# A two-layer hybrid encoder on one core: the four buffers of the sums of x at other addresses by 256 than the weights

## The chip, the core and the metric

The kernel runs on one core of one Trainium2 chip. The metric is the device time of one execution in microseconds (us), the median of several runs. Of the core's engines, the profile calls the matrix engine PE, and the part of it that loads the stationary operand PEld; VectorE is DVE, ScalarE is ACT, GpSimd is POOL, and SP issues most DMAs. All operands of a matmul lie in the on-chip memory, in 128 partitions. An address below is a byte offset inside a partition.

## The reference

Two layers work on 256 tokens of width 1024, all in float32. Each layer has a half-weighted SwiGLU block, an attention block with two groups of heads, and a second SwiGLU block. Shortened:

```python
def swiglu(h, w_gate, w_up, w_down):
    return (jax.nn.silu(h @ w_gate) * (h @ w_up)) @ w_down

for l in range(DEPTH):                      # 2
    x = x + 0.5 * swiglu(rms_norm(x, ffn1_norm[l]), ffn1_w_gate[l], ffn1_w_up[l], ffn1_w_down[l])
    h = rms_norm(x, mix_norm[l])
    qa, ka, va, qb, kb, vb = jnp.split(h @ w_in[l], SPLITS, axis=-1)
    out_a = windowed_gqa_sink(qa, ka, va, sink[l], slopes_a)
    out_b = differential_attention(qb, kb, vb, lam, slopes_b)
    out_b = (rms_norm(out_b, diff_subln[l]) * (1.0 - lam_init)).reshape(b, s, B_V_COLS)
    x = x + jnp.concatenate([out_a, out_b], axis=-1) @ w_out[l]
    x = x + 0.5 * swiglu(rms_norm(x, ffn2_norm[l]), ffn2_w_gate[l], ffn2_w_up[l], ffn2_w_down[l])
return rms_norm(x, final_norm)
```

The hidden width of a SwiGLU block is 2816: five groups of 512 columns and a rest of 256.

## The kernel before

**Matmuls in two halves.** Every float32 operand is split into a high and a low half of type float32r, which PE multiplies in one pass. A product a·b is three matmuls into one accumulator: high·high, low·high, high·low. The weights come by DMA into `raw` tiles of 8 KB a partition (six of them) and are split there by ScalarE (the cast to the high half) and VectorE (the difference to the low one) into tiles `w` of 4 KB. These share the pool `s4` (28 tiles) with the halves of x and of the hidden blocks, which are named `s` in the profile. In the SwiGLU blocks the activations are the stationary operand (128 columns, 512 bytes) and the weights the moving one (512 columns, 2 KB). PEld loads the next matmul's stationary operand while the present one streams.

**Seven products in place of eight.** For most groups of 512 columns `by_sevens` computes the gate and up projections of both token blocks by a scheme with seven products instead of eight: x and the weights are cut in two along the tokens and along the 1024 inputs, and sums of parts are multiplied. Four of the seven products take a sum of parts of x as the stationary operand. The three others take a quarter of x itself (`quarter`, in the pool `s4`). `make_sums` forms the four sums once per norm, and `high` and `low` write their halves: three of them into tiles with the tag `q` (three buffers), one into a tile with the tag `v` (one buffer). `summed(i)` hands them to `prod`, which issues 12 matmuls of 512 columns for one sum:

```python
        def prod(xo, w, acc=None):
            ...
                pe.matmul(acc, lhsT=xh, rhs=hi, start=first and k == 0, stop=False, skip_group_check=not first)
                pe.matmul(acc, lhsT=xl, rhs=hi, start=False, stop=False, skip_group_check=not first)
                pe.matmul(acc, lhsT=xh, rhs=lo, start=False, stop=k == 3, skip_group_check=not first)
```

Fifteen groups in the four SwiGLU blocks go this way (three in the first block, four in each other): 15 x 4 x 12 = 720 matmuls whose stationary operand is a sum.

**The same buffers in the attention block.** There the sums are not alive. `q_finish` puts the halves of the projected queries into the buffers with the tag `q`, and `scores` loads them as stationary operand in 64 rows, two matmuls side by side, against the keys (`blk()`, pool `s4`). `vB`, the values of the second head group, lies in the buffer with the tag `v` and is the moving operand of the product with the attention weights.

**Order.** PE's instructions stay in the order of the program; `ahead` and the tables `LEAD` say how early a weight is fetched and split. A scheduler that knows durations places the rest. None of that depends on an address.

**Where tiles lie.** A pool's tags follow one another in the order of their first use; a tag with n buffers takes n tiles in a row, each rounded up to 32 bytes. Taken modulo 256, the `raw` tiles, all tiles of `s4`, the five buffers of the tag `tmp`, and the buffers of `q` and `v` begin at 160; x itself (`xk`) and the identity (`ident`) begin at 128, `vA` at 32. Within a tile the operands start at multiples of 512 bytes. Behind `v` in the same pool lie small tiles of the attention block (`den_b`, `R`, `negm`, `vA` and others).

Of the kernel before, what the change touches and what calls it, by code (L numbers as in the profile page):

```python
# [9 lines left out]
F32 = mybir.dt.float32  # L10
F32R = mybir.dt.float32r
# [3 lines left out]
P = 128  # L15
# [31 lines left out]
def trunk(ctx: ExitStack, tc: tile.TileContext, x, n1, g1, u1, d1, nm, w_in, sink,  # L47
# [26 lines left out]
    tp = ctx.enter_context(tc.tile_pool(name="tp", bufs=1))  # L74
# [4 lines left out]
    def nm_(s):  # L79
        uid[0] += 1  # L80
        return f"{s}_{uid[0]}"
# [4 lines left out]
    def pair():  # L86
        return [ps.tile([P, 512], F32, tag="xy", bufs=2, name=nm_("xy")) for _ in range(2)]
# [6 lines left out]

    def tmp(tag="tmp", bufs=5, shape=(P, 2, 256), dt=F32):
        return tp.tile(list(shape), dt, tag=tag, bufs=bufs, name=nm_(tag))

    f = lambda t: t.bitcast(F32)

    def urgent():  # L100

        return tc.high_priority(300)
# [241 lines left out]
    class Norm:  # L344


        def __init__(self, g0, sums=True):
            self.g0, self.xs, self.sums = g0, [], sums
            self.xg, self.turned = [], []
            self.ss = tmp("nss", 2, (P, 2, 4))  # L350

        def squares(self, t, c, n):
            j_ = tmp("junk", 1, (P, 512))
            act.activation(j_[:, :n], xk[:, t, c:c + n], AF.Square, accum_out=self.ss[:, t, c // 256:c // 256 + 1])
# [34 lines left out]
        def make_sums(self):  # L389

            self.sm = []

            (t0, t1), (b0, b1) = [(t[:, :, 0:P], t[:, :, P:S]) for t in self.xg]

            def add(x, y, op):
                v = tmp().rearrange("p a (c s) -> p (a c) s", c=2)
                dve.tensor_tensor(v, x, y, op=op)
                return v

            def high(v):  # L400
                tag, n = ("q", 3) if len(self.sm) < 3 else ("v", 1)
                sm = tp.tile([P, 2, 512], F32R, tag=tag, bufs=n, name=nm_(tag)).rearrange("p a (c s) -> p (a c) s", c=2)
                act.copy(sm[:, :, 0:P], v)
                self.sm.append(sm)

            def low(i, v):
                dve.tensor_tensor(self.sm[i][:, :, P:S], v, f(self.sm[i][:, :, 0:P]), op=ALU.subtract)

            v = add(t1, t0, ALU.subtract)
            s1 = add(t1, b1, ALU.subtract)  # L410
            yield
            high(v)
            high(s1)
            yield
            low(0, v)
            s2 = add(t0, s1, ALU.subtract)
            low(1, s1)
            b0_ = add(b0, s2, ALU.subtract)
            yield
            high(b0_)  # L420
            high(s2)
            yield
            low(2, b0_)
            low(3, s2)
            yield
# [8 lines left out]
        def summed(self, i):  # L434
            return lambda k: (self.sm[i][:, k, 0:P], self.sm[i][:, k, P:S])
# [191 lines left out]
    def split(dst, src, scale=None):  # L627

        act.copy(dst[:, :, 0:S], src)
        dve.tensor_tensor(dst[:, :, S:512], src, f(dst[:, :, 0:S]), op=ALU.subtract)  # L630
# [331 lines left out]
    def mix(l, norm, nxt_norm):  # L962
# [10 lines left out]
        def whole(sl, sc=(1.0, 1.0)):  # L973

            t = tmp()
            for i, b in enumerate(sl):
                act.activation(t[:, i], b[:, S:512], AF.Copy, scale=sc[i])
            for i, b in enumerate(sl):
                dve.scalar_tensor_tensor(t[:, i], in0=b[:, 0:S], scalar=sc[i], in1=t[:, i], op0=ALU.mult, op1=ALU.add)
            dve.tensor_tensor(t, t, bc(norm.R), op=ALU.mult)  # L980
            return t

        def q_finish(sl, sc):
            q = tp.tile([P, 2, 512], F32R, tag="q", bufs=3, name=nm_("q"))
            with urgent():
                split(q, whole(sl, sc))
            return [q[:, 0], q[:, 1]]
# [54 lines left out]
        k_finish(whole(s0), 2, [("b", 0), ("b", 1)])  # L1042
        k_finish(whole(s1), 2, [("b", 2), ("b", 3)])
        q0 = q_finish(ngroup(norm, weights()), [qscB[:, 0:1], qscB[:, 1:2]])
        q1 = q_finish(ngroup(norm, weights()), [qscB[:, 2:3], qscB[:, 3:4]])
        tkv = whole(ngroup(norm, weights()))
        a_b = [soft_b(0, q0[0]), soft_b(1, q0[1])]
        k_finish(tkv, 1, ["a"])

        qA0 = q_finish(ngroup(norm, weights()), [qscA[:, 0:1], qscA[:, 1:2]])  # L1050
        a_b += [soft_b(2, q1[0]), soft_b(3, q1[1])]
        vsl = halves(bank())
# [16 lines left out]
        def keys_first_b(hp):  # L1069
            return keys_first(lambda kc, i: a_b[2 * hp + i // 2][:, i % 2, kc * P:(kc + 1) * P])  # L1070
# [3 lines left out]


        aT = [keys_first_b(0)]
        vB = tp.tile([P, 2, 512], F32, tag="v", bufs=1, name=nm_("v"))
        both = pair()
        vsl = both
        for k0 in (0, 4):  # L1080
# [123 lines left out]
    for l in range(DEPTH):  # L1204
        final = l == DEPTH - 1
        parts = ffn(norm, attention_constants, take_x, sevens=SEVEN[0]) if l == 0 else ffn(norm)
        norm_m = Norm(16 + l * 8, False)
        ffn_close(parts, norm_m)
        norm2 = Norm(32 + l * 8)
        mix(l, norm_m, norm2)  # L1210
        parts = ffn(norm2, final_gain if final else None, final=final)
        if not final:
            norm = Norm((l + 1) * 8)
            ffn_close(parts, norm)
# [75 lines left out]
```

## Time and profile before

| what | value |
|---|---|
| median of 3 runs | 909.28 us (909.23 to 909.46) |
| profiled execution, first to last instruction (span) | 907.5 us |
| granted clock of PE, mean | 0.999 |
| PE busy, its share of the span | 899.1 us, 99% |
| PEld / DVE / ACT / POOL busy | 751.0 / 785.9 / 609.8 / 63.2 us |
| share of PE in the chain of work that ended last | 98% |
| HBM read | 199 MB, 220 GB/s over the span |

The profiled execution has no other time of its own than the span; the median of the runs is 1.8 us above it.

A row of instructions names the output and the inputs by the program's tiles without their numbers: `ps<-w,q` is a matmul into a tile of the tag `ps`, with a weight `w` and a tile of the tag `q` as operands; then the rows and columns of the array in use, the shape of the moving operand, the count, the busy time in us, the mean of one in ns, and the idle time of the engine before them with what ended it. All rows have line 62, the line of the helper that issues for every engine, so groups are told apart by tile names. A matmul's recorded time ends after its result has drained, so consecutive matmuls overlap in the record, and the pace is read from their starts or from many of them together. The chain of waits follows the work that ended last back from the end, step by step.

### The profile page before, as it was taken

How to read it: one execution, taken by the hardware profiler on the slowest of the kernel's cores; microseconds unless marked ns; L12 is line 12 of the kernel's file. 1: busy time of each engine (PE TensorE's matmuls, PEld its weight loads, DVE VectorE, ACT ScalarE, POOL GpSimd, SP SyncE). 2: the span in 40 equal slices, each digit the busy share in tenths (PEclk: the TensorE clock that was granted, in tenths of full speed). 3: DMA queues.
4: the chain of work that ended last, by engine and by line, in shares of the span. 5: the costliest groups of instructions: out<-in, count | busy, mean ns of one | idle time of the engine just before them, and what ended most of it. 6: DMA issues, size and time to landing. Idle time of an engine off the chain costs nothing.

```text
span 907.5 us, 12030 instructions
## 1 busy us (share of the span) xinstructions
PE 899.1 (99%) x4468; PEld 751.0 (83%) x4468; DVE 785.9 (87%) x1069; ACT 609.8 (67%) x970; POOL 63.2 (7%) x79
## 2 busy tenths in 40 slices
PE   9999999999999999999999999999999999999997
PEld 7888888888888888888888888888888888888886
DVE  5968999879987899999778999988888978999894
ACT  6946677666776776677575776667667785776660
POOL 0401000000001001000000001000000000101011
PEclk9999999999999999999999999999999999999999
DMA  9998897954148798897976898899611786898731
GB/s 328 355 287 213 236 309 247 268 143 179 47 150 241 174 265 247 247 300 256 279 204 171 250 278 258 252 303 248 182 57 48 263 223 166 234 312 255 219 114 47
DMA packets 114331, 200.83 MB, mean 221 GB/s; under 512 B 3678, under 2 KB 31648, under 8 KB 114272
## 3 DMA queue, kind: packets, MB, share of 16 engines
q1 hardware_dynamic: 97616, 167.66, 54.4%
q0 software_dynamic: 16096, 31.75, 20.1%
q8 instruction: 35, 0.57, 0.2%
q10 hardware_dynamic: 560, 0.66, 0.2%
q14 instruction: 24, 0.20, 0.1%
HBM read 199.00 MB, written 1.05 MB: 220 GB/s over the span
## 4 chain that ended last, share of the span: by engine, by line
PE 98%; DMA 1%; issue 0%; SPq 0%; DVE 0%; POOLq 0%; POOL 0%
PE ps L62 73%; PE xy L62 25%; DMA xk<-in_x_dram 1%; SPq L172 0%; DVE s L62 0%; DVE xk L62 0%; POOLq L1285 0%; POOL rf L62 0%; SPq L469 0%; SPq L465 0%; DVE tot L62 0%; DVE tmp L62 0%
## 5 line engine op out<-in xcount | busy, mean ns | idle before, releaser
L62 DVE TENSOR_TENSOR w<-raw,w 128x1024 fp32r<-128x1024 f32 (+1 forms) x458 | 476.4, 1097 | 34.6 <-ACT w L62 33.2
L62 PE MATMUL ps<-w,s 128*128 128x512 f32 (+1 forms) x2046 | 473.6, 389 | 0.0
L62 PEld LDWEIGHTS ps<-w,s 128*128 128x128 f32 x2046 | 379.9, 188 | 78.7 <-issue 0.8
L62 ACT CAST w<-raw 128x1024 fp32r<-128x1024 f32 (+1 forms) x457 | 403.9, 954 | 54.0 <-DVE raw L62 38.7
L62 PE MATMUL xy<-w,s 128*128 128x512 f32 x528 | 125.8, 392 | 0.0
L62 PEld LDWEIGHTS xy<-w,s 128*128 128x128 f32 x528 | 98.2, 188 | 20.4
L62 PE MATMUL xy<-w,q 128*128 128x512 f32 x360 | 88.1, 393 | 0.0
L62 PEld LDWEIGHTS xy<-w,q 128*128 128x128 f32 x360 | 66.5, 188 | 13.3
L62 PE MATMUL ps<-s,w 128*128 128x512 f32 (+1 forms) x384 | 69.8, 338 | 0.0
L62 DVE TENSOR_TENSOR raw<-raw,raw 128x2048 f32<-128x2048 f32 x30 | 68.6, 2288 | 0.5
L62 POOL DMA_DIRECT2D raw<-in_ffn_w_up_dram x30 | 38.9, 1313 | 430.1 <-DVE w L62 264.9
L62 PEld LDWEIGHTS ps<-s,w 128*128 128x128 f32 x384 | 58.6, 188 | 8.5
L62 ACT ACTIVATE s<-ps,gcol 128x256 fp32r<-128x256 f32 (+1 forms) x80 | 31.4, 479 | 34.0 <-PE ps L62 34.0
L62 ACT CAST s<-ps 128x512 fp32r<-128x512 f32 x36 | 20.4, 592 | 43.2 <-PE ps L62 43.0
L62 PE MATMUL ps<-w,q 128*128 128x512 f32 x180 | 43.2, 389 | 0.0
L62 PE MATMUL ps<-w,v 128*128 128x512 f32 x180 | 43.2, 389 | 0.0
L62 DVE TENSOR_TENSOR s<-ps,s 128x512 fp32r<-128x512 f32 x36 | 24.1, 686 | 19.5 <-ACT s L62 19.3
L62 PEld LDWEIGHTS ps<-w,v 128*128 128x128 f32 x180 | 33.8, 188 | 7.0
L62 PEld LDWEIGHTS ps<-w,q 128*128 128x128 f32 x180 | 33.8, 188 | 7.0
L62 ACT ACTIVATE s<-s,negm 128x256 f32<-128x256 f32 x64 | 31.8, 498 | 5.3 <-DVE negm L62 5.3
L62 ACT COPY ps<-ps 128x512 f32<-128x512 f32 x15 | 8.6, 570 | 34.4 <-PE ps L62 34.4
L62 DVE SCALAR_TENSOR_TENSOR s<-ps,gcol,s 128x256 fp32r<-128x256 f32 x48 | 20.3, 477 | 13.0 <-ACT s L62 12.9
(131 smaller groups left out, 584.3 us busy)
## 6 DMA issues: line engine op xcount, KB each, us to landing
raw<-in_ffn_w_down_dram SPq DMA_DIRECT2D x44, 1024.0 KB, 7.0
raw<-in_ffn_w_gate_dram SPq DMA_DIRECT2D x39, 1024.0 KB, 7.7
raw<-in_ffn_w_up_dram SPq DMA_DIRECT2D x39, 1024.0 KB, 7.1
raw<-in_ffn_w_up_dram POOLq DMA_DIRECT2D x30, 1024.0 KB, 10.0
raw<-in_w_in_dram SPq DMA_DIRECT2D x14, 1024.0 KB, 6.7
raw<-in_ffn_w_gate_dram SPq DMA_DIRECT2D x8, 512.0 KB, 7.9
raw<-in_ffn_w_up_dram SPq DMA_DIRECT2D x8, 512.0 KB, 8.9
raw<-in_w_in_dram SPq DMA_DIRECT2D x8, 512.0 KB, 6.0
```

What stands on the lines that cost most here:

```text
L62: ins = issue(*a, **k)
```

## The change

The tiles of the sums are made by a new helper, `summed`. The tag `q` gets tiles of 1048 columns instead of 1024, of which the first 1024 are used, so that its three buffers lie 4192 bytes apart. Ahead of the first buffer of each tag stands a tile that nothing uses, of 32 bytes for `q` and 96 bytes for `v`. By that the three buffers of `q` begin 32, 128 and 224 bytes behind the weights' address by 256, and the one of `v` 160 bytes behind. What follows `v` in the pool lies 416 bytes further on. The three places that made these tiles call the helper. The instructions are the same.

```diff
+    placed = set()
+
+    def summed(tag, n, dt=F32R):
+
+        if tag not in placed:
+            placed.add(tag)
+            tp.tile([P, 8 if tag == "q" else 24], F32, tag="edge_" + tag, bufs=1, name="edge_" + tag)
+        t = tp.tile([P, 1024 + 24 * (tag == "q")], dt, tag=tag, bufs=n, name=nm_(tag))
+        return t[:, 0:1024].rearrange("p (a n) -> p a n", a=2)
...
             def high(v):
                 tag, n = ("q", 3) if len(self.sm) < 3 else ("v", 1)
-                sm = tp.tile([P, 2, 512], F32R, tag=tag, bufs=n, name=nm_(tag)).rearrange("p a (c s) -> p (a c) s", c=2)
+                sm = summed(tag, n).rearrange("p a (c s) -> p (a c) s", c=2)
                 act.copy(sm[:, :, 0:P], v)
...
         def q_finish(sl, sc):
-            q = tp.tile([P, 2, 512], F32R, tag="q", bufs=3, name=nm_("q"))
+            q = summed("q", 3)
...
-        vB = tp.tile([P, 2, 512], F32, tag="v", bufs=1, name=nm_("v"))
+        vB = summed("v", 1, F32)
```

## The prediction

> **What bounds the kernel now.** I read the page's first and fourth parts first, to see which engine sets the end.
>
> ```profile
> span 907.5 us, 12030 instructions
> PE 899.1 (99%) x4468; PEld 751.0 (83%) x4468; DVE 785.9 (87%) x1069; ACT 609.8 (67%) x970; POOL 63.2 (7%) x79
> PEclk9999999999999999999999999999999999999999
> PE 98%; DMA 1%; issue 0%; SPq 0%; DVE 0%; POOLq 0%; POOL 0%
> ```
>
> The matrix engine is the path: 98% of the chain of waits, at a clock that never drops. So an edit pays only if a matmul on PE, or the load of its stationary operand (PEld), takes another time. The change issues the same instructions, so the only question is what an address does to one. Next come the groups of PE's instructions with their shapes kept apart.
>
> ```profile
> L62 PE MATMUL ps<-w,s 128*128 128x512 f32 x2010 | 469.3, 390 | 0.0
> L62 PE MATMUL xy<-w,q 128*128 128x512 f32 x360 | 88.1, 393 | 0.0
> L62 PE MATMUL ps<-s,w 128*128 128x512 f32 x192 | 68.2, 398 | 0.0
> L62 PE MATMUL ps<-w,q 128*128 128x512 f32 x180 | 43.2, 389 | 0.0
> L62 PE MATMUL ps<-w,v 128*128 128x512 f32 x180 | 43.2, 389 | 0.0
> L62 PE MATMUL ps<-s,q 64*128 64x256 f32 x144 | 10.7, 289 | 0.0
> L62 PE MATMUL ps<-s,vA 128*64 128x256 f32 x64 | 7.3, 382 | 0.0
> ```
>
> The sums of x (q and v) are the stationary operand of 360 + 180 + 180 = 720 matmuls, the weights (w) their moving operand. The mean of one row hides gaps, so the chain of waits in order of time gives the true pace: start, length, instructions.
>
> ```profile
> 41.28 10.88 PE xy L62 x48
> ...
> 100.20 10.88 PE ps L62 x48
> ```
>
> 10.88 us / 48 = 226.7 ns from one start to the next, and the recorded 389 ns is that pace plus 162 ns in which the result drains beside the next matmul. 720 x 226.7 ns = 163 us, 18% of the span, is all that the sums' loads lie beneath.
>
> **The change part by part.** Nothing is removed and no wait is added. Three things move: the four buffers of the sums, the small tiles allocated behind them, and so the distance between what PE loads and what it streams.
>
> First, what is the distance now? By the sizes of the pools, taken in order and each tile rounded up to 32 bytes, the raw weights, the blocks of the split weights and of x, tmp, q and v all start at 160 modulo 256: relation 0 throughout. xk and ident start at 128, which is 224 from the weights. The table by tile for q, in the stretch 107.6 to 120 us, shows how even relation 0 is (shortest, median and longest ns):
>
> ```profile
> L62 PE MATMUL ps<-w,q x12: 389/389/389, 108.2 to 110.7; 128*128 128x512 f32 x12
> L62 PE MATMUL xy<-w,q x12: 389/389/389, 110.9 to 113.4; 128*128 128x512 f32 x12
> ```
>
> q lies 256 bytes off the weights modulo 512 and the halves of x lie 0 off; both take 389 ns. So a distance of 256 does nothing. That is why only the remainder by 256 can count, and no row here shows 32, 128 or 160 beneath this kind of matmul.
>
> The largest gain that a better relation can bring is the cost of the load itself: no relation is better than no load. The trace has such a matmul. At 232.55 us the last matmul ahead of the scores streams with no load beneath it, because the next stationary operand (64 rows of q) is loaded only after it. The first two lines are the load engine's timeline around it, the third the groups in 232.80 to 232.86 us, where this matmul is alone.
>
> ```profile
> 231.88 0.64 PEld L62 LDWEIGHTS xy<-w,s 128*128 128x128 f32 x3
> 232.87 0.65 PEld L62 LDWEIGHTS ps<-s,q 64*128 64x128 f32 x10 [0.35 <-issue]
> L62 PE MATMUL xy<-w,s 128*128 128x512 f32 x1 | 0.4, 388 | 0.0
> ```
>
> 388 ns without a load against 389 with one: at relation 0 a load costs the stream 1 ns. Gain at most 720 x 1 ns = 0.7 us. With the shortest of 360 in the row below (387) it would be 720 x 2 = 1.4 us.
>
> ```profile
> L62 PE MATMUL xy<-w,q x360: 387/389/497, 66.4 to 860.7; 128*128 128x512 f32 x180
> ```
>
> The Trainium skill (TensorE: Matmul & The Clock Gate, Step-by-step: what each phase is for) says that PE reads the streamed and the loaded operand through two independent ports and that "Loading the next tile's weights doesn't steal SBUF read bandwidth from the running matmul." By that rule the change gives exactly nothing; the 388 against 389 agrees to 1 ns.
>
> The rule of two free ports is not the whole of it, though. Another relation does appear once under a 512-column matmul: where transposes follow, the load of xk (224) or of a hidden block s (0) rides beneath the last matmul. Both windows below hold one matmul alone, 277.65 to 277.68 us with xk loaded, 160.72 to 160.77 us with s:
>
> ```profile
> L62 PE MATMUL ps<-w,s 128*128 128x512 f32 x1 | 0.4, 392 | 0.0
> ...
> L62 PE MATMUL xy<-w,s 128*128 128x512 f32 x1 | 0.4, 395 | 0.0
> ```
>
> Relation 224 is 3 ns shorter than relation 0 here. It is a load in transpose form, so its price (4 to 7 ns over 388) is not that of an ordinary load; but it shows a load can stretch the stream, and gives the loss's bounds. If an ordinary load at a new relation cost 4 ns instead of 1, the sum is 720 x 3 = 2.2 us; with 7 instead of 1, 720 x 6 = 4.3 us. The dearest mean in the trace for 512 columns is 398 (weights stationary, two sizes in turn), still at relation 0: 720 x 9 = 6.5 us, the far end. I take 0, because an ordinary load is nearest to the 388/389 pair, and keep -1.4 and +6.5.
>
> The scores use q as stationary operand too, in 64 rows, two at a time. Here are the shortest, median and longest, then the attention product with v moving, then the one with vA:
>
> ```profile
> L62 PE MATMUL ps<-s,q x144: 275/278/383, 214.1 to 686.1; 64*128 64x256 f32 x144
> L62 PE MATMUL xy<-s,q x48: 276/280/280, 215.0 to 668.9; 64*128 64x256 f32 x48
> L62 PE MATMUL xy<-v,s x64: 275/275/275, 247.2 to 696.6; 128*128 128x128 f32 x64
> L62 PE MATMUL ps<-s,vA x64: 379/379/430, 252.7 to 701.8; 128*64 128x256 f32 x64
> ```
>
> 192 score matmuls are 96 pairs; median over shortest is 3 to 4 ns, so at most 96 x 4 = 0.4 us either way. v as moving operand: 64 without any spread, 0. vA, which the longer buffers push 416 bytes on, already lies off its partner (32 against 160) and its median is its shortest: 0.
>
> The sums are written by ScalarE and VectorE. xk at 224 stands for a shifted operand:
>
> ```profile
> L62 DVE TENSOR_TENSOR q<-tmp,q 128x512 fp32r<-128x512 f32 x20 | 13.7, 684 | 2.9 <-ACT q L62 2.9
> L62 DVE TENSOR_TENSOR xk<-xk,ps 128x512 f32<-128x512 f32 x17 | 11.2, 681 | 2.2 <-PE ps L62 2.2
> ```
>
> 681 against 684 ns: nothing. The 24 writes cover themselves behind PE; uncovered, 24 x 3 ns is 0.07 us. DMAs, queues and small tiles keep their instructions and count 0. Of 31 us in a stage of products VectorE is busy 29.7:
>
> ```profile
> 82.00:113.00 31.00, 31.00 (x143) 25.74 (x142) 29.68 (x28) 22.03 (x27) 2.58 (x2) 1.00 0.88 243
> ```
>
> So 1.3 us of 31 is the room in which a faster PE can run before VectorE, which splits the weights, is late next. A gain of 1.4 us over fifteen such groups uses 0.1 of it.
>
> The sum: 907.5 us (span) + 0 = 907.5. The span and the median of the runs, 909.28, differ by 1.8 us that lie around the span and stay: 909.3.
>
> **The rivals.** *Faster: the relation costs the whole stretch, not just the load's 1 ns.* The vA product streams 256 columns in two passes, 512 steps, at another relation (128), and takes 379 ns against 389. If the 10 ns between them were a clash of equal relations, and all four new relations avoided it, 720 x 10 = 7.2 us go: 902.1. With half the buffers freed, 905.7. For it speaks that vA is off its partner, that xk is 3 ns better than s, and that everything lies on relation 0 now. Against it: the matmul without a load still takes 388, so 9 of the 10 ns stay where nothing can clash, and vA is another format (fp32 in two passes). VectorE's room carries it: 48 x 10 ns is 0.5 of 1.3 us a group.
>
> The Trainium skill (TensorE: Matmul & The Clock Gate, Wait — 56ns, not 53.3ns?) gives 215.7 ns as the pace of warm matmuls of 512 columns, measured back to back; against 226.7 here that leaves 11 ns unexplained, and by it 720 matmuls at that pace would give 909.3 - 7.9 = 901.4 us as an estimate. The trace does not reach that pace anywhere with 512 columns of this format.
>
> *Slower: relation 0 is the good one.* Load and stream now walk the same addresses in step and lock into 226.7 ns; at 32, 128, 160 or 224 each load meets the stream out of step in all its blocks. The price is 3 to 6 ns a matmul from the two transpose loads, +2.2 to +4.3 us: 911.5 to 913.6. It decides from 2.5 ns a matmul on (1.8 us). For it speaks that PE's pace is so even now that it looks locked, and the 398 ns row, where the rhythm is another. Against: xk at 224 was better, not worse.
>
> *The relations cancel.* Two of the four gain 2 ns, two lose 3, on 180 matmuls each by the count of buffers: -0.7 + 1.1 = +0.4 us, 909.7. It falls under no change.
>
> *The change does not do what it says* would need a tile to be placed otherwise than the sizes say; q and v lying at relation 0 still would give 909.3, no change as well.
>
> **How the numbers follow.** 0.2% of 909.3 is 1.8 us, about what a measurement of this kernel can tell from no change. No change (the load costs 1 ns, or the parts cancel): 0.47, and it is the forecast, 909.3, its own range 907.9 to 911. Faster by the stretch, in whole or part (902.1 to 907.4): 0.33; the new relations have not been seen, and the one that was, 224, helped. Slower (911.2 to 915.8): 0.20. The range takes in the whole no-change case, most of the faster one and the nearer half of the slower one: 902.5 to 912.0.
>
> **What would show it.** Right: the chain still gives 10.88 us for 48 matmuls, the rows of q and v read 389, and the load beneath them 188 ns. The faster rival shows as q and v rows at 379 to 387 with the rows of s unchanged at 389, and groups shorter than 10.88 us where a sum is stationary. The slower one shows as 392 to 395 in those rows only. If one of the four buffers does better than another, the q row spreads between its shortest and longest while v (160) keeps a single value. Should the rows of s move as well, my reading that only a matmul's own neighbours count is wrong; should q and v rows drop while the time stays, the gain has gone into a wait on VectorE.

## The result, and the profile after

The changed kernel takes 914.33 us (914.31 to 914.88, 3 runs) against 909.28 us before: a ratio of 1.0056, 95% interval 1.0036 to 1.0076. It is slower by 5.05 us, and the forecast of no change was wrong. Its profiled execution has a span of 912.5 us against 907.5.

The first and fourth parts of the page after, in the lines that answer to those shown of before:

```profile
span 912.5 us, 12030 instructions
PE 904.8 (99%) x4468; PEld 752.2 (82%) x4468; DVE 786.0 (86%) x1069; ACT 609.9 (67%) x970; POOL 62.8 (7%) x79
PEclk9999999999999999999999999999999999999999
PE 99%; issue 0%; DVE 0%; POOLq 0%; POOL 0%
```

The same instructions at the same clock, and PE is still the path. PE is busy 5.7 us longer, and the span grew by 5.0. The 0.7 us between them lies in the first 9 us: there this execution's first six matmuls of s took 2.69 us in place of 1.83, and before waited 0.7 us for x where this one did not. The two nearly cancel, and a run without any loss (e10 below, 2.56 us for the same six) starts as this one does. No other engine changed by more than 1.2 us. PE's groups by shape tell which matmuls it is:

```profile
L62 PE MATMUL ps<-w,s 128*128 128x512 f32 x2010 | 470.9, 391 | 0.0
...
L62 PE MATMUL xy<-w,q 128*128 128x512 f32 x360 | 90.0, 399 | 0.0
L62 PE MATMUL ps<-s,w 128*128 128x512 f32 x192 | 68.2, 398 | 0.0
L62 PE MATMUL ps<-w,v 128*128 128x512 f32 x180 | 44.4, 395 | 0.0
L62 PE MATMUL ps<-w,q 128*128 128x512 f32 x180 | 44.3, 395 | 0.0
```

The three rows in which a sum is the stationary operand rose from 393, 389 and 389 ns to 399, 395 and 395: 6 ns for each of 720 matmuls, 4.3 us. The big row of s rose by 1.6 us, from 390 to 391 ns; 0.9 us of that are its first six matmuls, and the rest is taken up below. The weights as stationary operand (398) did not move. How even the sums' rows were is gone, in the table by tile (shortest, median, longest):

```profile
L62 PE MATMUL ps<-w,q x180: 390/395/404, 77.4 to 862.9; 128*128 128x512 f32 x180
...
L62 PE MATMUL ps<-w,v x180: 388/394/399, 83.0 to 868.5; 128*128 128x512 f32 x180
```

The loads beneath them, in the same table:

```profile
L62 PEld LDWEIGHTS ps<-w,q x180: 187/188/192, 77.2 to 862.6; 128*128 128x128 f32 x180
```

The timeline of PE around three products of one group shows it best. Each line is a run of matmuls: start, length up to the last one's drained end, tiles, count. Before, all distances 0:

```profile
108.20 2.88 PE L62 MATMUL ps<-w,q 128*128 128x512 f32 x12
110.92 2.88 PE L62 MATMUL xy<-w,q 128*128 128x512 f32 x12
113.64 2.88 PE L62 MATMUL ps<-w,v 128*128 128x512 f32 x12
116.36 4.92 PE L62 MATMUL ps<-w,s 128*128 128x512 f32 x21
```

After, at distances 224, 128 and 160 from the weights by 256:

```profile
108.53 2.96 PE L62 MATMUL ps<-w,q 128*128 128x512 f32 x12
111.33 2.96 PE L62 MATMUL xy<-w,q 128*128 128x512 f32 x12
114.12 2.95 PE L62 MATMUL ps<-w,v 128*128 128x512 f32 x12
116.92 4.28 PE L62 MATMUL ps<-w,s 128*128 128x512 f32 x18
```

From start to start a product took 2.72 us and takes 2.79 to 2.80: 226.7 ns a matmul became 233. PEld's load beneath them still reads 188 ns at the median, as before, so the load is not slower; the stream above it is.

To see where the rest went I took the starts of all matmuls from the trace, in program order. Against a pace of 226.67 ns, and against the same sums of before, the matmuls inside the 60 products lost 3.9 us, those at their borders 0.4, and matmuls of s against weights 0.8. These last have all distances at 0. They follow a product and need up to eight matmuls to find 227 ns again (234, 235, 225, 230, 236, 229, 232, 231, 227 ns in one case), 27 ns on average after each of the 30 products that matmuls of s follow. Together 5.1 us, the whole of the span's growth.

### The profile page after: what moved, and what is told of

The parts are those of the page before. It is cut to its first block, busy times and chain, and to the rows that moved or that the text cites. A ratio compares the mean times of both kernels' runs of the same rounds, so it can differ in the third digit from the quotient of the medians.

```text
span 912.5 us, 12030 instructions
## 1 busy us (share of the span) xinstructions
PE 904.8 (99%) x4468; PEld 752.2 (82%) x4468; DVE 786.0 (86%) x1069; ACT 609.9 (67%) x970; POOL 62.8 (7%) x79
## 4 chain that ended last, share of the span: by engine, by line
PE 99%; issue 0%; DVE 0%; POOLq 0%; POOL 0%
PE ps L62 73%; PE xy L62 25%; DVE s L62 0%; DVE xk L62 0%; POOLq L1295 0%; POOL rf L62 0%; DVE wake L62 0%; DVE tot L62 0%; DVE tmp L62 0%
## 5 line engine op out<-in xcount | busy, mean ns | idle before, releaser
L62 PE MATMUL xy<-w,q 128*128 128x512 f32 x360 | 90.0, 399 | 0.0
```

The costliest lines, as they stand in the source:

```text
L62: ins = issue(*a, **k)
```

## The experiments

The runs are called e1 to e11. The table gathers what those with the sums at other distances say of the pace: the mean time from one start to the next within the products of a sum, the first matmul after a gap left out, by the distance of the sum's buffer from the weights by 256. Every figure is from the trace of the run named.

A trace holds no addresses, so which of its three buffers a product of `q` takes is inferred: the sums are taken to go through them in turn, in the order first, third, second. Two things in the runs bear it out. Only so do the products at 128, which two runs have, show the same steps from start to start in both (241, 232, 231, 232, 228, 230, 233 ns in the changed kernel and in e3); and only so is the buffer that keeps 226.7 ns in e4 the one at 16, as e9 with all buffers at 16 wants it.

| distance in bytes | ns a matmul | run |
|---|---|---|
| 0 | 226.7 (v), 227.2 (q) | before |
| 4, 16, 48, 80 | 232.3, 227.5, 233.3, 232.0 | e4 |
| 8, 24, 104, 200 | 230.7, 230.5, 233.2, 231.2 | e6 |
| 32, 128, 160, 224 | 232.9, 232.8, 233.5, 233.2 | changed kernel |
| 64, 96, 128, 192 | 233.4, 233.7, 232.9, 229.8 | e3 |
| 144, 176, 208, 240 | 231.6, 230.6, 231.7, 228.1 | e5 |
| 16 alone | 226.7 (v), 228.0 (q) | e9 |
| 144 alone | 226.7 (v), 228.6 (q) | e11 |

### Distance or place: everything moved together (e1)

```diff
+    const.tile([P, 24], F32, name="edge")
     xk = const.tile([P, 2, D], F32, name="xk")
```

> Built on the kernel before: an unused tile of 96 bytes at the very start moves every other tile by 96 bytes, so weights, blocks of x, q and v begin at 0 instead of 160 by 256, and every distance between them stays as it was (0). Theory of the distance (a load costs the stream more when it does not lie on the streamed operand's address by 256): rows of q, v and s stay at 389 ns, 10.88 us for 48 matmuls, 909.3 us. Rival, theory of the place (a load wants its own start at 160, or off a 64-byte boundary): every load is now as off as those of three of the four buffers in the changed kernel, so some 3300 matmuls take 6 to 7 ns more, +20 to +23 us, 930 us.

909.05 us, ratio 0.9997 (0.9987 to 1.0006). The groups of PE by shape:

```profile
L62 PE MATMUL xy<-w,q 128*128 128x512 f32 x360 | 88.1, 393 | 0.0
L62 PE MATMUL ps<-w,q 128*128 128x512 f32 x180 | 43.2, 389 | 0.0
L62 PE MATMUL ps<-w,v 128*128 128x512 f32 x180 | 43.2, 389 | 0.0
```

Row for row as before. All operands start at 0 by 256 here, on a 64-byte boundary as three of the four buffers of the changed kernel did, and it costs nothing. The place theory falls; what counts is the distance.

### The small tiles behind v alone (e2)

```diff
+    tail_moved = []
...
                 act.copy(sm[:, :, 0:P], v)
+                if len(self.sm) == 3 and not tail_moved:
+                    tail_moved.append(tp.tile([P, 104], F32, tag="edge", bufs=1, name="edge"))
```

> The kernel before with one part of the change alone: an unused tile of 416 bytes behind v, so that the small tiles behind it (vA, R, negm and others) lie where the changed kernel has them, and q and v stay at 0. Theory of the distance between the sums and the weights: 909.3 us, rows of q and v 389. Rival (the moved small tiles carry the loss): 914.3 us with 389 in the rows of q and v.

909.23 us, ratio 0.9998 (0.9989 to 1.0008), rows of q and v at 393, 389 and 389 as before. The moved small tiles, vA among them, carry nothing; the loss belongs to the sums' buffers.

### Other distances (e3 to e6)

In e3, the same helper with other paddings, `q` at 64, 128 and 192, `v` at 96:

```diff
-            tp.tile([P, 8 if tag == "q" else 24], F32, tag="edge_" + tag, bufs=1, name="edge_" + tag)
-        t = tp.tile([P, 1024 + 24 * (tag == "q")], dt, tag=tag, bufs=n, name=nm_(tag))
+            tp.tile([P, 16 if tag == "q" else 24], F32, tag="edge_" + tag, bufs=1, name="edge_" + tag)
+        t = tp.tile([P, 1024 + 16 * (tag == "q")], dt, tag=tag, bufs=n, name=nm_(tag))
```

> The changed kernel with other paddings: the buffers of q lie 64, 128 and 192 bytes from the weights by 256, the one of v 96. Theory of the distance, period 256: none of them is 0, so all rows stay at 393 to 396 and the time at 914.3 (913 to 915). Rival, period 64 (a block of 64 bytes): q falls back to 389 in all three buffers, only v stays high, 910.5. Rival, period 32 of odd multiples (32, 96, 160, 224 are bad, 64 and 192 good, 128 bad by chance): q falls by two thirds of its loss, 911.5.

913.29 us, ratio 1.0042 (1.0026 to 1.0059). 64, 96 and 128 cost as much as the distances of the change, so periods of 32 and 64 fall. 192 was not foreseen: 229.8 ns, about half the loss. In PE's timeline its product is the first here (192, 128, 96; start to start 2.75, 2.80, 2.80 us):

```profile
108.73 2.92 PE L62 MATMUL ps<-w,q 128*128 128x512 f32 x12
111.48 2.96 PE L62 MATMUL xy<-w,q 128*128 128x512 f32 x12
114.28 2.96 PE L62 MATMUL ps<-w,v 128*128 128x512 f32 x12
117.08 0.62 PE L62 MATMUL ps<-w,s 128*128 128x512 f32 x2
```

Distances below 32 bytes need an operand that starts inside its tile. In e4 `q` is at 16, 48 and 80, `v` at 4:

```diff
-            tp.tile([P, 8 if tag == "q" else 24], F32, tag="edge_" + tag, bufs=1, name="edge_" + tag)
+            if tag == "v":
+                tp.tile([P, 40], F32, tag="edge_v", bufs=1, name="edge_v")
-        t = tp.tile([P, 1024 + 24 * (tag == "q")], dt, tag=tag, bufs=n, name=nm_(tag))
-        return t[:, 0:1024].rearrange("p (a n) -> p a n", a=2)
+        t = tp.tile([P, 1024 + 8], dt, tag=tag, bufs=n, name=nm_(tag))
+        o = 4 if tag == "q" else 1
+        return t[:, o:o + 1024].rearrange("p (a n) -> p a n", a=2)
```

> The changed kernel with distances below 32 bytes: q at 16, 48 and 80, v at 4 (the operand starts inside its tile). Theory of equal addresses in the strict sense: v at 4 is already off and its row stays at 394 to 396; 914.3. Theory of blocks (load and stream clash by blocks of 16, 32 or 64 bytes): v at 4 lies in the same block for most of its length and its row falls to 389 to 391; q at 16 falls too if the block is larger than 16 and stays high if not; 48 and 80 stay high; 912 to 913.

912.87 us, ratio 1.0039 (1.0024 to 1.0054). PE's timeline in one group, with the products at 48, 16 and 4:

```profile
349.28 2.96 PE L62 MATMUL ps<-w,q 128*128 128x512 f32 x12
352.08 2.89 PE L62 MATMUL xy<-w,q 128*128 128x512 f32 x12
354.80 2.94 PE L62 MATMUL ps<-w,v 128*128 128x512 f32 x12
357.58 1.77 PE L62 MATMUL ps<-w,s 128*128 128x512 f32 x7
```

16 takes 2.72 us, the pace of distance 0, and 4 takes 2.78. Neither theory had that: blocks would have made 4 the better one. Two more sets, by the same edit with other numbers, one run each (e5, `q` at 176, 208, 240 and `v` at 144; e6, `q` at 8, 104, 200 and `v` at 24):

> The changed kernel with other distances, all multiples of 16: q at 176, 208 and 240, v at 144. Theory of a rhythm (PE's pace falls into one of a few steady patterns of stream and load, and the distance by 256 picks which): 226.7 ns only near 0, so q at 240 (16 short of 0) reads 389 like 16 did, 176, 208 and 144 read 392 to 396, 912 to 913.5. Rival, the 16-byte theory (odd multiples of 16 alone are harmless; 48 and 80 were bad by chance of what ran ahead of them): most rows of q and v at 389, about 910.

911.98 us beside 909.17 before (seven runs, 908.89 to 910.55). 240 falls back near 227 (228.1 ns) as 16 had, the rest stay above 230.

> The changed kernel with distances that are multiples of 8 only: q at 8, 104 and 200, v at 24. Rhythm theory: 8 lies between 4 (bad) and 16 (good), 24 between 16 (good) and 32 (bad), so these two tell how wide the good place is; 104 and 200 read 392 to 396; 911.5 to 914. Rival (16-byte lines: what is no multiple of 16 is bad): all four at 392 or more, 913 to 914.5. A distance better than 0 would read below 389; neither theory expects one.

912.74 us beside 909.17. All four are high, 104 most (233.2). So in these sets the good places are 0 and the steps of 16 beside it. None of the nineteen other distances was faster than 0.

### One load in three off (e7)

The high halves of the sums stay at 0, the low halves lie 32 bytes off:

```diff
-                sm = tp.tile([P, 2, 512], F32R, tag=tag, bufs=n, name=nm_(tag)).rearrange("p a (c s) -> p (a c) s", c=2)
-                act.copy(sm[:, :, 0:P], v)
+                t = tp.tile([P, 1088], F32R, tag=tag, bufs=n, name=nm_(tag))
+                sm = [t[:, o:o + 512].rearrange("p (k s) -> p k s", k=4) for o in (0, 520)]
+                act.copy(sm[0], v)
...
```

> Built on the kernel before: the high halves of the sums stay at 0, the low halves lie 32 bytes off (highs of a buffer first, 8 unused columns, then the lows; buffers 4352 bytes apart). In each three matmuls the loads are high, low, high, so one of three loads is off. Theory of the load beneath (the stream is stretched by the load of the next matmul's operand): the first of each three, under which the low half is loaded, takes 6 to 8 ns more, the others little; 720 / 3 x 7 = +1.7 us, 911. Rival, theory of the own operand (a matmul whose own stationary operand lies off takes longer): the second of each three takes more and the first none. Third, no stretch unless several loads in a row are off: 909.3 and 389 in all rows.

913.32 us, ratio 1.0047 (1.0032 to 1.0062): 4.15 us, most of what it cost to have all loads off (5.05). In the stretch from 111.04 us three windows hold the matmuls of one triple: the first with a neighbour, the second and the third alone (groups by shape):

```profile
L62 PE MATMUL xy<-w,q 128*128 128x512 f32 x1 | 0.4, 400 | 0.0
...
L62 PE MATMUL xy<-w,q 128*128 128x512 f32 x1 | 0.4, 389 | 0.0
...
L62 PE MATMUL xy<-w,q 128*128 128x512 f32 x1 | 0.4, 395 | 0.0
```

The starts give 239, 228 and 233 ns, over and over. The longest is the first of the three, the one beneath which the off load runs; the second, whose own operand lies off, is almost at the old pace. Such a turn of three is not proof by itself, since the product at 160, with all its loads off alike, has one too (232, 238, 230 ns). The way into a product settles it. In each of the fifteen groups one product follows matmuls of s at 226.7 ns. In the changed kernel the last of these s, whose own operand is at 0 while the first off load runs beneath it, already takes 232 to 235 ns, in all fifteen. In e7, where that first load is at 0, it takes 226 or 227, and the product's first matmul, beneath which the first low half is loaded, takes 235, again in all fifteen. So it is the load beneath that stretches the stream, and the theory of the own operand falls. But the third of each three is late too, with nothing off beneath it, and the mean of a turn is 233.3 ns. The loss is not so many nanoseconds an off load; the three fall into another rhythm.

### A rhythm: what a product comes from (e9 to e11)

In e5 the fifteen products at distance 144 went two ways. Here are two groups of that run, in PE's timeline; the third line of each is the product at 144:

```profile
108.22 2.88 PE L62 MATMUL ps<-w,q 128*128 128x512 f32 x12
110.94 2.94 PE L62 MATMUL xy<-w,q 128*128 128x512 f32 x12
113.72 2.96 PE L62 MATMUL ps<-w,v 128*128 128x512 f32 x12
116.52 0.86 PE L62 MATMUL ps<-w,s 128*128 128x512 f32 x3
...
798.99 2.90 PE L62 MATMUL xy<-w,q 128*128 128x512 f32 x12
801.73 2.88 PE L62 MATMUL ps<-w,v 128*128 128x512 f32 x12
804.45 1.30 PE L62 MATMUL ps<-w,s 128*128 128x512 f32 x5
```

2.80 us in the first, 2.72 in the second. The first came from a product at 208 that ran at 232 ns, the second from one at 240 that had reached 226.7. If the state decides, all four buffers at 144 must do well, since most products then follow matmuls of s at 226.7 ns. I tested that (e11), 16 alone (e9), and as a control the same long tiles at a distance of 0 (e10). The edit for 16 is below, shortened, with the unused tiles ahead dropped; the control has `o = 0`, and 144 keeps an unused tile of 128 bytes ahead of `q`:

```diff
-        t = tp.tile([P, 1024 + 24 * (tag == "q")], dt, tag=tag, bufs=n, name=nm_(tag))
-        return t[:, 0:1024].rearrange("p (a n) -> p a n", a=2)
+        t = tp.tile([P, 1088], dt, tag=tag, bufs=n, name=nm_(tag))
+        o = 4
+        return t[:, o:o + 1024].rearrange("p (a n) -> p a n", a=2)
```

> All four buffers 144 bytes from the weights by 256. In the run with 176, 208, 240 and 144 the fifteen products at 144 went two ways: the eleven that came after a product at 231 to 235 ns ran at 233 ns, the four that came after one at 226.7 ns kept 226.7. Theory of a state (the pace in which a product starts decides whether this distance holds it): now three of four products of a group follow products of s at 226.7 ns or one another, and keep it; 909.3 to 911. Rival (the distance alone decides, and 144 costs 5 ns on average): 720 x 5 = 3.6 us, 912.5 to 913.5.

910.46 us, ratio 1.0011 (1.0001 to 1.0020): a loss of 1.1 us where the distance alone would give 3.6. PE's timeline, first after transposes, then the same three products as above:

```profile
96.79 0.60 PE L62 MATMUL xy<-ident,s 128*128 128x128 f32 x4
97.14 3.05 PE L62 MATMUL xy<-w,q 128*128 128x512 f32 x12
100.03 1.31 PE L62 MATMUL ps<-w,s 128*128 128x512 f32 x5
...
108.20 2.88 PE L62 MATMUL ps<-w,q 128*128 128x512 f32 x12
110.92 2.88 PE L62 MATMUL xy<-w,q 128*128 128x512 f32 x12
113.64 2.88 PE L62 MATMUL ps<-w,v 128*128 128x512 f32 x12
116.36 0.84 PE L62 MATMUL ps<-w,s 128*128 128x512 f32 x3
```

All 45 products that follow s or another sum hold 226.7 ns (2.72 us a product). Of the 15 that follow transposes, where PE's pace starts anew, 14 run at 230 to 238 ns to their end. So the same address costs 0 or 5 to 6 ns by the pace in which it is met.

> All four buffers of the sums 16 bytes from the weights by 256. Of fifteen products at 16 bytes in the run with 16, 48, 80 and 4, twelve kept 226.7 ns. Theory of the rhythm that a distance of 16 can hold: rows of q and v at 389 but for the products that follow transposes, 909.3 to 910.5. Rival (anything but 0 costs): 913 to 914 as with the other distances.

909.98 us, ratio 1.0006 (0.9996 to 1.0015), not to be told from no change. The 45 products after s or another sum hold 226.7 ns; of the fifteen after transposes, nine run at 231 to 236 ns to near their end.

> The tiles of the sums 4352 bytes long instead of 4096, so that the same padding is there and every distance is 0 by 256 (the buffers lie at different multiples of 256). Theory of the distance by 256: 909.3, rows at 389. Rival (the padding itself, longer steps between buffers): 913 to 914.

909.30 us, ratio 0.9999 (0.9990 to 1.0008), rows at 393, 389 and 389. Padding by itself, or a distance of a whole multiple of 256, costs nothing.

### The same on every matmul (e8)

All 28 tiles of the pool of the weights' and activations' halves lie 4128 bytes apart instead of 4096:

```diff
-        return s4.tile([P, 2, 512], dt, tag="s4", name=nm_("s4"))
+        return part(dt, "s4")
+
+    def part(dt, name, a=2):
+        t = s4.tile([P, 1032], dt, tag="s4", name=nm_(name))
+        return t[:, 0:1024].rearrange("p (a n) -> p a n", a=a)
...
-        hi, lo = [s4.tile(list(shape), F32R, tag="s4", name=nm_("w")) for _ in range(2)]
+        hi, lo = [part(F32R, "w", shape[1]) for _ in range(2)]
```

> Built on the kernel before: all 28 tiles of the pool s4 (split weights, halves of x and of the hidden blocks) lie 4128 instead of 4096 bytes apart, so that the distance between any load and any stream is some multiple of 32, 0 in one of eight. Theory of the distance: 7/8 of some 3300 loads under 512 columns cost 5 to 7 ns more, +14 to +20 us, 923 to 929, and the rows of s, not only those of q and v, read 393 to 396. Rival (only the sums' buffers matter, through something else that they share): 909 to 914.

924.85 us, ratio 1.0173 (1.0156 to 1.0189): 15.7 us for 32 bytes a tile. The groups of PE show it in the rows of s now:

```profile
L62 PE MATMUL ps<-w,s 128*128 128x512 f32 x2010 | 479.7, 395 | 0.0
L62 PE MATMUL xy<-w,s 128*128 128x512 f32 x528 | 128.4, 396 | 0.0
L62 PE MATMUL xy<-w,q 128*128 128x512 f32 x360 | 89.6, 397 | 0.0
L62 PE MATMUL ps<-s,w 128*128 128x512 f32 x192 | 68.4, 397 | 0.0
```

390 and 392 became 395 and 396. From the starts, 3159 matmuls of 512 columns take 231.9 ns on average, against 227.0 before. What each single distance cost here is not shown, as the trace does not tell which of the 28 tiles a matmul used. The weights as stationary operand (398 before, 397 now) had another rhythm already, 231 to 233 ns for 512 columns although all distances were 0, and lost almost nothing (0.2 us).

## Why the prediction was wrong

**What held.** PE is the path, and an address alone decided the case; VectorE, DMAs, the writes of the sums (683 ns at the median for the tile q before, 682 after), the scores, vB and the moved small tiles counted nothing, as predicted. A whole multiple of 256 does nothing (e10). The bound on a gain held too: a better distance could bring at most what the load costs at 0, and none of the nineteen others brought anything.

**The step that failed** is the first term of the sum, the price of a load at a new distance, taken as 0 within -1.4 to +6.5 us. It measured 6 ns a matmul, 4.3 us with the borders, plus 0.8 us that the sum had no term for, in matmuls of s behind each product. I drew 0 from the pair of 388 ns without a load and 389 with one. Both rows are of distance 0. The pair bounds what could be won by moving away from 0; it says nothing of what could be lost. To go on from "a load costs 1 ns here" to "an ordinary load costs 1 ns" was the mistake. The evenness of 389/389/389, which the prediction named in favour of the slower rival, got no weight in the sum. A second reading failed with it, that only a matmul's own neighbours count: its sign was to be rows of s that move, and the 0.8 us behind the products are that.

**The row that misled** was the load of xk, 392 ns at 224 against 395 at 0. It spoke against the slower rival and for the faster one. The changed kernel has 224 as one of its distances, and there an ordinary load brings 395 (233.2 ns). What a load in transpose form cost said nothing of an ordinary one.

**The rivals.** The slower one was right in direction and near in mechanism, and put at 0.20: distance 0 is the good one, though 16 and 144 can keep its pace. Its price of 3 to 6 ns from the transposes, 911.5 to 913.6 us, was short by the carry into s: its upper end and 0.8 us make 914.4. That this end met the measured 6 ns is luck, since it was read from transposing loads. The rival guessed that load and stream lock; e7 and e11 show that there is a rhythm and that a product can keep or lose it, but not that the two walk the same addresses in step. The far end of the sum, 915.8, held the result, but I drew the range to 912.0 only. The faster rival's 9 to 10 ns between this format and vA's are not a clash of equal addresses: no distance averaged less than 226.7 ns, and the row of vA read 382 ns before and after, although its own distance changed from 128 to 32. That distances cancel each other is refuted by the table.

The Trainium skill (TensorE: Matmul & The Clock Gate, Step-by-step: what each phase is for) was quoted with two independent ports, by which a load takes nothing from the stream. The one matmul without a load bears that out to 1 ns at distance 0. At most other distances it does not hold: 226.7 ns became 233 with nothing but the load's address changed. Here the measurement decides.

**What stays open.** Why the remainder by 256 counts, and why 16 and 240 are milder than 8 and 24, no run tells. Whether some distance allows less than 226.7 ns was tried at twenty places out of 64 and found nowhere.

## What to carry to other kernels

Where PE is the path, give the stationary and the moving operand addresses that agree by 256 bytes, and pad tiles by multiples of 256 only; 32 bytes a tile in the shared pool cost 1.7% here. This was measured with float32r operands, 128 columns loaded and 512 streamed, the activations stationary; with the weights stationary e8 lost 0.2 us, and other types were not tried. Before a change that only moves buffers, take all operands' addresses by 256 as part of the change. And read a row without any spread as a lock that may break: bound the loss with rows that have the new condition, not with rows that lack it.

## What the runs showed of the hardware

PE's pace for 512 columns is here a state and not a price. With the activations stationary and all distances 0 it returned to 226.7 ns from every start seen, within three to ten matmuls after transposes; at 16, 144 and 240 it is held if met, but not always found; at 4, 32, 48, 64, 80, 104, 128 and 224 it is lost at once or after one matmul. The other patterns repeat too: 239, 228, 233 with one load in three off, 226, 229, 232 at 192, 231 and 236 in turn at 64. Several of them, at quite different distances, average 233.3 ns, 6.7 ns above 226.7. And a product out of step costs its neighbours as well, 27 ns on average for each return to the old rhythm.
